# Latent products of a hybrid diffusion block: the order of the high-weight and low-weight matmuls

## The chip, the cores and the metric

The kernel runs on one core of one Trainium2 chip. The metric is the device time of one execution in microseconds. Before the change it was 2398.35 us, the median of three runs (2396.97 to 2398.81).

## The reference, cut to what matters

One layer of a diffusion backbone works on 256 latent tokens and 256 context tokens, D_MODEL = 2048. A token mixer (a bidirectional Mamba-2 scan with a gate z, a Conformer branch, two branch gates, an output projection) is followed by a SwiGLU FFN with 5632 hidden channels. Only the latent stream is returned.

```python
proj = h @ w_in                     # h: (b, L, 2048); columns z | x, B, C | dt | glu | gates
...
y_a = rmsnorm(y * jax.nn.silu(z), ssm_norm) @ w_proj_a            # 4096 -> 2048
u, v = jnp.split(glu, 2, axis=-1)
cf = jax.nn.silu(layernorm(cf_conv(u * jax.nn.sigmoid(v)), cf_ln_g, cf_ln_b))
y_b = cf @ w_proj_b                                               # 2048 -> 2048
out = (jax.nn.sigmoid(g_a) * y_a + jax.nn.sigmoid(g_b) * y_b) @ w_out
...
def swiglu(h, w_gate, w_up, w_down):
    return (jax.nn.silu(h @ w_gate) * (h @ w_up)) @ w_down        # 2048 -> 5632 -> 2048
```

All inputs are float32. The products that the change touches are those of the latent tokens alone: the columns z, glu and gates of `w_in`, and `w_proj_a`, `w_proj_b`, `w_ffn_gate`, `w_ffn_up`.

## The kernel before, in words

**Three products for one.** TensorE works on float32r operands. A float32 product is made of three: weights and activations are each split into a rounded part (high) and the remainder (low), and high x high, high x low and low x high are added up. An activation tile holds both parts side by side, `[P, k, 2, 256]`: 256 tokens high, then 256 tokens low.

**A unit of weights.** `unit_cols` (line 118) loads 512 KB: four k-tiles (`UK` = 4, 128 rows each) by 256 output columns. SP issues the DMA into a float32 tile w (6 buffers). `split` (line 110) then lets ACT round it into the tile wh (line 114; the high weights, 4 buffers) and DVE subtract to the tile wl (line 115; the low weights, 4 buffers). Both are emitted with the priority of an instruction 450 places earlier.

**A product with the weights stationary.** `mm_unit` (line 132, its branch for `wd` = 0) does, for each of the two 128-column halves j of a unit: four matmuls with a high weight tile, each over 512 columns (256 tokens high, 256 tokens low; line 152), then four with a low weight tile over the 256 columns of the high activations (line 154). The two results of one output half stand in one PSUM bank, columns 0 to 255 and 256 to 511. In the last unit of a product the last high matmul is held back to the end of the half (line 156). Each matmul has a weight load of its own. In the text below, H is a matmul of lines 152 and 156 and lo is one of line 154; a unit is thus H4 lo4 into one bank and H4 lo4 into the next.

**The end of a product.** `fold` (line 200) takes a bank out: an ACT copy of the one half (line 203), then a DVE add of the other half (line 204). Only then is the bank free. There are four such banks (`accp`, line 78), taken in turn in pairs by `acc2()`.

**Where such products run.** `zpair` (line 743) and `gpair` (line 788) lie between the steps of the scan (about 240 to 970 us); after each unit they yield, and the scan puts its own steps there. `pair` (line 846) does the glu columns, the rest of the gates, `w_proj_b` and `w_proj_a` (about 970 to 1540 us; the first two column groups of `w_proj_a` in a loop of their own, line 970). In all of these the next product takes the other two banks. In the FFN (line 1060, about 1655 to 2144 us) a group j of 256 hidden channels takes all four banks: two for the gate (ag), two for the up product (au), and their units alternate: gate, up, gate, up, eight units to a group. The first group does its gate product in another way (`mm_half`). `xpair` and `bcpair` (512-column matmuls throughout, but for the C half) and `chunks` (`w_out`, `w_down`: activations stationary, lines 174 to 177) are other forms.

**What sets the order.** A planner sorts the instructions while it builds the program: on each engine it takes, of those that are ready in its own account of time, the one with the earliest priority. On the chip each engine then runs its list strictly in that order. Behind every unit a `hook` (line 565) may emit a step of `modvec` (line 519), a background job on DVE (lines 533 to 537, tile mac) that multiplies and adds rows of `w_mod` as their DMAs come.

## Time and profile before

| | before |
|---|---|
| median of 3 runs | 2398.35 us |
| the profiled execution's own time | 2399.29 us |
| its span (first to last instruction) | 2397.6 us |
| mean granted TensorE clock | 0.994 |
| PE busy | 2337.8 us, 98% |
| PE weight loads busy | 1968.7 us, 82% |
| DVE busy | 1633.7 us, 68% |
| ACT busy | 1252.8 us, 52% |

PE is TensorE's matmul row and PEld its weight-load row. Matmuls are pipelined, so the busy time of PE is a union of overlapping rows; what a matmul costs in a stream is the distance from its start to the next one's start, not its own duration. The distances below are taken so.

### The profile page before, as it was taken

The page shows a single profiled execution, that of the slowest core. Times are in us where ns is not written, and L with a number is a line of the kernel's source. Part 1 is how long each engine was busy: PE and PEld are TensorE (multiplying, and loading weights), DVE is VectorE, ACT ScalarE, POOL GpSimd, SP SyncE. Part 2 cuts the span into 40 slices and gives each one's busy share as a digit, 9 for nine tenths or more (in the row PEclk, how much of TensorE's full clock was granted, in tenths as well). Part 3 has the DMA queues.
Part 4 walks back from the last instruction along what each step waited for, and adds up shares of the span by engine and source line. Part 5 has one row for each costly group of instructions (what it writes and reads, how often), then busy time and mean ns, then how long its engine had stood idle before and what let it go on. Part 6 is the DMA issues. An engine that isn't in the chain of part 4 may idle for free.

```text
span 2397.6 us, 34659 instructions
## 1 busy us (share of the span) xinstructions
PE 2337.8 (98%) x13180; PEld 1968.7 (82%) x13180; DVE 1633.7 (68%) x2099; ACT 1252.8 (52%) x1934; POOL 126.9 (5%) x149
## 2 busy tenths in 40 slices
PE   6899999999999999999999999998999999999998
PEld 3668788888888788888888888888888888888888
DVE  4559867676676776889878776767666566655554
ACT  4335766666566675654575444445444444444433
POOL 1000000100000000011300000000000000000000
PEclk9999999999999999999999999999999999999999
DMA  9884545546455566888799987885777677767553
GB/s 276 273 272 135 134 133 150 159 134 159 131 150 162 147 189 192 280 254 284 227 286 300 287 275 249 299 289 169 224 230 222 214 226 225 227 201 247 194 193 115
DMA packets 444848, 510.46 MB, mean 213 GB/s; under 512 B 17944, under 2 KB 391927, under 8 KB 443529
## 3 DMA queue, kind: packets, MB, share of 16 engines
q1 hardware_dynamic: 438904, 488.75, 66.7%
q0 software_dynamic: 5216, 18.41, 2.2%
q8 instruction: 103, 1.69, 0.3%
q10 hardware_dynamic: 560, 1.08, 0.1%
q14 instruction: 65, 0.52, 0.1%
HBM read 499.51 MB, written 8.67 MB: 212 GB/s over the span
## 4 chain that ended last, share of the span: by engine, by line
PE 89%; DMA 5%; DVE 2%; ACT 2%; issue 1%; SPq 1%; DVEq 0%; ACTq 0%
PE acc L152 34%; PE acc L154 18%; PE acc L144 6%; PE acc L145 5%; PE acc L147 5%; PE acc L177 4%; PE acc L174 4%; PE acc L175 4%; DMA w<-in_w_mod_dram 3%; PE acc L156 2%; DMA w<-in_w_in_dram 2%; PE ss L716 1%; PE ss L413 1%; DMA cs<-cs_d 1%; PE ss L686 1%
## 5 line engine op out<-in xcount | busy, mean ns | idle before, releaser
L115 DVE TENSOR_TENSOR wl<-w,wh 128x1024 fp32r<-128x1024 f32 (+3 forms) x702 | 847.1, 1210 | 486.6 <-ACT wh L114 484.4
L114 ACT CAST wh<-w 128x1024 fp32r<-128x1024 f32 (+3 forms) x702 | 717.7, 1024 | 742.2 <-PE acc L152 349.6
L152 PE MATMUL acc<-hx,wh 128*128 128x512 f32 x1556 | 433.0, 397 | 0.0
L152 PE MATMUL acc<-h,wh 128*128 128x512 f32 x1290 | 356.6, 395 | 1.9 <-DVE fe L204 1.9
L152 PEld LDWEIGHTS acc<-hx,wh 128*128 128x128 f32 x1556 | 271.9, 189 | 40.8 <-issue 2.2
L154 PEld LDWEIGHTS acc<-hx,wl 128*128 128x128 f32 x1664 | 254.8, 188 | 37.6 <-DVE wl L115 2.1
L144 PE MATMUL acc<-hx,wh 128*128 128x512 f32 x656 | 266.3, 407 | 3.0 <-ACT wh L114 2.6
L154 PE MATMUL acc<-hx,wl 128*128 128x256 f32 x1664 | 265.1, 281 | 1.4 <-DVE wl L115 1.4
L145 PE MATMUL acc<-hx,wh 128*128 128x512 f32 x656 | 259.2, 395 | 0.2 <-DVE hx L440 0.2
L152 PEld LDWEIGHTS acc<-h,wh 128*128 128x128 f32 x1290 | 225.5, 189 | 34.0 <-DVE fe L204 2.6
L154 PEld LDWEIGHTS acc<-h,wl 128*128 128x128 f32 x1376 | 211.5, 189 | 29.7
L537 DVE SCALAR_TENSOR_TENSOR mac<-w,silc,mac 128x1024 f32<-128x1024 f32 x120 | 154.7, 1289 | 104.7 <-DMA w<-in_w_mod_dram 104.0
L154 PE MATMUL acc<-h,wl 128*128 128x256 f32 x1376 | 219.5, 281 | 0.0
L147 PE MATMUL acc<-hx,wl 128*128 128x512 f32 x656 | 183.2, 392 | 0.0
L144 PEld LDWEIGHTS acc<-hx,wh 128*128 128x128 f32 x656 | 124.2, 189 | 38.1 <-ACT wh L114 8.2
L175 PE MATMUL acc<-wh,hid 128*128 128x512 f32 (+1 forms) x440 | 146.8, 347 | 0.0
L174 PE MATMUL acc<-wh,hid 128*128 128x512 f32 (+1 forms) x440 | 146.8, 347 | 0.0
L145 PEld LDWEIGHTS acc<-hx,wh 128*128 128x128 f32 x656 | 124.3, 190 | 26.3 <-issue 1.4
L147 PEld LDWEIGHTS acc<-hx,wl 128*128 128x128 f32 x656 | 123.3, 188 | 27.2 <-issue 0.7
L152 PE MATMUL acc<-yg,wh 128*128 128x512 f32 x496 | 136.3, 395 | 0.0
L177 PE MATMUL acc<-wl,hid 128*128 128x512 f32 (+1 forms) x440 | 109.5, 347 | 0.0
L667 ACT ACTIVATE cs<-cs,ncs 128x128 f32<-128x128 f32 x256 | 81.6, 390 | 34.6 <-DMA cs<-cs_d 30.9
(331 smaller groups left out, 2795.0 us busy)
## 6 DMA issues: line engine op xcount, KB each, us to landing
w<-in_w_in_dram SPq DMA_DIRECT2D x248, 512.0 KB, 4.5
w<-in_w_mod_dram SPq DMA_DIRECT2D x192, 512.0 KB, 4.8
w<-in_w_ffn_gate_dram SPq DMA_DIRECT2D x88, 512.0 KB, 4.5
w<-in_w_ffn_up_dram SPq DMA_DIRECT2D x88, 512.0 KB, 4.5
w<-in_w_ffn_down_dram SPq DMA_DIRECT2D x88, 512.0 KB, 3.7
w<-in_w_proj_a_dram SPq DMA_DIRECT2D x64, 512.0 KB, 5.0
w<-in_w_in_dram SPq DMA_DIRECT2D x74, 256.0 KB, 3.8
cs<-cs_d SPq DMA_DIRECT2D x32, 512.0 KB, 5.8
```

What stands on the lines that cost most here:

```text
L114: A.copy(out=hi[:, :n], in_=t[:, :n])
L115: V.tensor_tensor(out=lo[:, :n], in0=t[:, :n], in1=hi[:, :n].bitcast(F32), op=ALU.subtract)
L144: E.matmul(o, wj(hi, k), act(kofs + k)[:, 0, :ncol], start=kofs + k == kbeg, stop=False)
L145: E.matmul(o, wj(hi, k), act(kofs + k)[:, 1, :ncol], start=False, stop=False)
L147: E.matmul(o, wj(lo, k), act(kofs + k)[:, 0, :ncol], start=False, stop=last and k == nk - 1)
L152: E.matmul(o2, wj(hi, k), act(kofs + k)[:, :, :T], start=kofs + k == kbeg, stop=False)
L154: E.matmul(o[:, :T], wj(lo, k), act(kofs + k)[:, 0, :T], start=False, stop=last and not hold)
L174: E.matmul(o, act(kofs + k)[:, 0, s], hi[:, k], start=kofs + k == 0, stop=False)
L175: E.matmul(o, act(kofs + k)[:, 1, s], hi[:, k], start=False, stop=False)
L177: E.matmul(o, act(kofs + k)[:, 0, s], lo[:, k], start=False, stop=kofs + k == kend - 1)
L537: V.scalar_tensor_tensor(out=ac, in0=wt, scalar=silc[:, k - 1:k], in1=ac, op0=ALU.mult, op1=ALU.add)
L667: A.activation(out=t4[:, r, j], in_=t4[:, r, j], func=AF.Identity, bias=ncs[:, cc, r * 64 + hs + j:r * 64 + hs + j + 1])
```

## The change

Two units are taken together. `mm_run` emits all H of the first unit (both halves), then all H of the second, then all lo of the first and of the second, then the held-back H of those units that end their product. In a product of one pair of banks (`cols_run`: z, glu, gates, `w_proj_b`, `w_proj_a`) the two units are neighbours in k; in the FFN they are the gate's and the up product's unit of the same k. Both units are loaded and split before the first matmul. The generator yields once ahead of the second unit's H and once at the end, so the number of yields and hooks stays the same; in the FFN both hooks stand behind the run. `xpair`, `bcpair`, `chunks`, the context stage and the first FFN group's gate keep their order.

```diff
+    def mm_run(us, kend, act):
+        def wide(a, j, hi, k, kk):
+            E.matmul(a[j].rearrange("p (h t) -> p h t", h=2), hi[:, k, j * P:(j + 1) * P], act(kk)[:, :, :T],
+                     start=kk == 0, stop=kk == kend - 1)
+        for n, (a, hi, lo, kofs) in enumerate(us):
+            if n == len(us) - 1:
+                yield
+            for j in range(2):
+                for k in range(UK):
+                    if kofs + k < kend - 1:
+                        wide(a, j, hi, k, kofs + k)
+        for a, hi, lo, kofs in us:
+            for j in range(2):
+                for k in range(UK):
+                    E.matmul(a[j][:, :T], lo[:, k, j * P:(j + 1) * P], act(kofs + k)[:, 0, :T], start=False, stop=False)
+        for a, hi, lo, kofs in us:
+            if kofs + UK == kend:
+                for j in range(2):
+                    wide(a, j, hi, UK - 1, kend - 1)
+
+    def cols_run(a, w, c0, ktot, act):
+        for k0 in range(0, ktot, 2 * UK):
+            us = [(a, *unit_cols(w, k, UK, [(c0, 256)]), k) for k in (k0, k0 + UK)]
+            yield from mm_run(us, ktot, act)
+            yield
...
         def zpair(g, j, res):
             a = acc2()
-            for k0 in range(0, KD, UK):
-                hi, lo = unit_cols(w_in, k0, UK, [(g * 512 + j * 256, 256)])
-                mm_unit(a, hi, lo, UK, k0, KD, [0, 0], hxa)
-                yield
+            yield from cols_run(a, w_in, g * 512 + j * 256, KD, hxa)
...
-    def pair(w, c0, ktot, act, hook=None, whole=0):
+    def pair(w, c0, ktot, act, hook):
         a = acc2()
-        for k in range(0, ktot, UK):
-            m = min(UK, ktot - k)
-            hi, lo = unit_cols(w, k, m, [(c0, 256)])
-            mm_unit(a, hi, lo, m, k, ktot, [whole] * 2, act, ncol=T if whole else 512)
-            if hook is not None:
-                hook()
+        for _ in cols_run(a, w, c0, ktot, act):
+            hook()
         return a
...
         first = [acc2(), acc2()]
         for k0 in (0, KD):
             for j in range(2):
-                for k in range(k0, k0 + KD, UK):
-                    hi, lo = unit_cols(w_pa, k, UK, [(j * 256, 256)])
-                    mm_unit(first[j], hi, lo, UK, k, 2 * KD, [0, 0], yact)
+                for k in range(k0, k0 + KD, 2 * UK):
+                    us = [(first[j], *unit_cols(w_pa, kk, UK, [(j * 256, 256)]), kk) for kk in (k, k + UK)]
+                    for _ in mm_run(us, 2 * KD, yact):
+                        hook()
                     hook()
...
             for k0 in range(0, KD, UK):
-                for w, a in ((w_gate, ag), (w_up, au)):
-                    if j or a is au:
-                        hi, lo = unit_cols(w, k0, UK, [(j * 256, 256)])
-                        mm_unit(a, hi, lo, UK, k0, KD, [0, 0], h2a)
-                        hook()
+                us = [(a, *unit_cols(w, k0, UK, [(j * 256, 256)]), k0)
+                      for w, a in ((w_gate, ag), (w_up, au)) if j or a is au]
+                for _ in mm_run(us, KD, h2a):
+                    pass
+                for _ in us:
+                    hook()
```

`gpair` changes as `zpair` does.

## Rows read from the trace of the kernel before

**Rows 1.** The page: the busy time of each engine (us, share of the span, number of instructions).
```profile
PE 2337.8 (98%) x13180; PEld 1968.7 (82%) x13180; DVE 1633.7 (68%) x2099; ACT 1252.8 (52%) x1934; POOL 126.9 (5%) x149
```
**Rows 2.** The page: the chain of work that ended last, by engine.
```profile
PE 89%; DMA 5%; DVE 2%; ACT 2%; issue 1%; SPq 1%; DVEq 0%; ACTq 0%
```
**Rows 3.** The timeline of PE at the end of one FFN group and the start of the next (start us, us, engine, line, operation, out<-in, form, count): the last matmul of each of the four banks, the next group's first, and the last matmul of the first bank one group later.
```profile
1892.00 0.39 PE L156 MATMUL acc<-h,wh 128*128 128x512 f32 x1
1893.40 0.39 PE L156 MATMUL acc<-h,wh 128*128 128x512 f32 x1
1894.80 0.39 PE L156 MATMUL acc<-h,wh 128*128 128x512 f32 x1
1896.20 0.39 PE L156 MATMUL acc<-h,wh 128*128 128x512 f32 x1
1896.43 1.09 PE L152 MATMUL acc<-h,wh 128*128 128x512 f32 x4
1897.36 0.63 PE L154 MATMUL acc<-h,wl 128*128 128x256 f32 x4
...
1914.44 0.39 PE L156 MATMUL acc<-h,wh 128*128 128x512 f32 x1
```
**Rows 4.** The timeline of PE in an `xpair` product: 512-column matmuls in a row, long after the last shorter one.
```profile
781.67 0.39 PE L145 MATMUL acc<-hx,wh 128*128 128x512 f32 x1
...
786.43 0.39 PE L152 MATMUL acc<-hx,wh 128*128 128x512 f32 x1
```
**Rows 5.** The same in another `xpair` product, just behind four 128-column transposes; of the rows between, each is one 512-column matmul.
```profile
404.04 0.60 PE L607 MATMUL tp<-ident,xc 128*128 128x128 f32 x4
404.39 0.48 PE L144 MATMUL acc<-hx,wh 128*128 128x512 f32 x1
404.71 0.39 PE L145 MATMUL acc<-hx,wh 128*128 128x512 f32 x1
...
406.10 0.39 PE L145 MATMUL acc<-hx,wh 128*128 128x512 f32 x1
406.33 0.85 PE L147 MATMUL acc<-hx,wl 128*128 128x512 f32 x3
```
**Rows 6.** The timeline of PE in the last chunk of `w_down`: 256-column matmuls in a long row.
```profile
2378.27 0.28 PE L174 MATMUL acc<-wh,hid 128*128 128x256 f32 x1
...
2379.23 0.64 PE L177 MATMUL acc<-wl,hid 128*128 128x256 f32 x4
```
**Rows 7.** The timeline of ACT over the group boundary of rows 3 (in brackets: idle time before it, and what ended it).
```profile
1892.43 0.37 ACT L203 COPY fe<-acc 128x256 f32<-128x256 f32 x1 [0.83 <-PE acc L156]
1893.83 1.05 ACT L114 CAST wh<-w 128x1024 fp32r<-128x1024 f32 x1 [1.03 <-PE acc L156]
1894.78 0.82 ACT L203 COPY fe<-acc 128x256 f32<-128x256 f32 x2
1896.51 0.64 ACT L1078 ACTIVATE fe<-fe 128x512 f32<-128x512 f32 x1 [0.90 <-DVE fe L204]
1897.04 1.04 ACT L114 CAST wh<-w 128x1024 fp32r<-128x1024 f32 x1
1897.98 0.36 ACT L203 COPY fe<-acc 128x256 f32<-128x256 f32 x1
```
**Rows 8.** The timeline of DVE over the same boundary.
```profile
1892.84 0.42 DVE L204 TENSOR_TENSOR fe<-fe,acc 128x256 f32<-128x256 f32 x1
1894.91 1.23 DVE L115 TENSOR_TENSOR wl<-w,wh 128x1024 fp32r<-128x1024 f32 x1 [1.66 <-ACT wh L114]
1896.06 0.75 DVE L204 TENSOR_TENSOR fe<-fe,acc 128x256 f32<-128x256 f32 x2
1896.72 1.28 DVE L537 SCALAR_TENSOR_TENSOR mac<-w,silc,mac 128x1024 f32<-128x1024 f32 x1
1898.11 1.23 DVE L115 TENSOR_TENSOR wl<-w,wh 128x1024 fp32r<-128x1024 f32 x1
1899.26 0.41 DVE L204 TENSOR_TENSOR fe<-fe,acc 128x256 f32<-128x256 f32 x1
```
**Rows 9.** Who waited for whom, 1660 to 2150 us (us in total, times, longest): PE's one line, and ACT's longest.
```profile
PE acc L152 <- DVE fe L204: 1.9, 1, 1.9
...
ACT wh L114 <- PE acc L152: 161.7, 103, 2.2
```
**Rows 10.** That one wait, between the FFN's first two groups: DVE, PE, and the granted clock by stretch (start:end, us, busy of PE, PEld, DVE, ACT, POOL, then the clock, DMA share, GB/s).
```profile
1670.77 1.29 DVE L537 SCALAR_TENSOR_TENSOR mac<-w,silc,mac 128x1024 f32<-128x1024 f32 x1 [1.63 <-DMA w<-in_w_mod_dram]
1671.97 0.41 DVE L204 TENSOR_TENSOR fe<-fe,acc 128x256 f32<-128x256 f32 x1
...
1667.53 1.09 PE L152 MATMUL acc<-h,wh 128*128 128x512 f32 x4
...
1672.44 1.19 PE L152 MATMUL acc<-h,wh 128*128 128x512 f32 x4 [1.95 <-DVE fe L204]
...
1672.50:1676.00 3.50, 3.50 (x13) 2.94 (x14) 3.47 (x5) 0.62 (x1) 0.00 (x0) 0.66 0.89 290
```
**Rows 11.** The timeline of PE at the start of `w_proj_b`, where the order that the program was written in would be H4 lo4 H4 lo4.
```profile
1268.43 1.62 PE L152 MATMUL acc<-cfx,wh 128*128 128x512 f32 x6 [2.63 <-DVE cfx L945]
1269.89 0.65 PE L154 MATMUL acc<-cfx,wl 128*128 128x256 f32 x4
1270.38 0.63 PE L152 MATMUL acc<-cfx,wh 128*128 128x512 f32 x2
1270.84 0.63 PE L154 MATMUL acc<-cfx,wl 128*128 128x256 f32 x4
```
**Rows 12.** Groups of instructions on DVE from 1667 to 2144 us: the background job's three lines (count, busy us, mean ns, idle before them).
```profile
L537 DVE SCALAR_TENSOR_TENSOR mac<-w,silc,mac 128x1024 f32<-128x1024 f32 x29 | 37.2, 1284 | 25.5 <-DMA w<-in_w_mod_dram 25.3
...
L535 DVE TENSOR_TENSOR mac<-mac,w 1x1024 f32<-1x1024 f32 x1 | 1.2, 1206 | 0.0
L533 DVE TENSOR_SCALAR mac<-w,silc 128x1024 f32<-128x1024 f32 x1 | 0.8, 755 | 1.1 <-DMA gr_d<-mac 1.1
```
**Rows 13.** PE's waits in the scan stage, 240 to 970 us, the four longest.
```profile
PE ss L686 <- DVE cs L679: 2.1, 2, 1.8
PE tp L607 <- ACT btok L629: 1.0, 1, 1.0
PE ss L686 <- PE acc L145: 0.8, 1, 0.8
PE ss L716 <- DVE y L722: 0.3, 1, 0.3
```

More of the change, by code (lines that the diff above doesn't have):

```diff
@@ L790, in gpair @@
             a = acc2()
-            for k0 in range(0, KD, UK):
-                hi, lo = unit_cols(w_in, k0, UK, [(OFF_GLU + j * 256, 256)])
-                mm_unit(a, hi, lo, UK, k0, KD, [0, 0], hxa)
-                yield
+            yield from cols_run(a, w_in, OFF_GLU + j * 256, KD, hxa)
             early.append(fold(a, xct().rearrange("p (i t) -> p i t", i=2)))
```

## The prediction

> **What bounds the kernel now.** I read the page first: PE is busy 98% of the span, no other engine over 82%, and PE's weight loads are on the same engine [rows 1]. The chain that ended last says the same: PE 89%, DMA 5% [rows 2]. So a microsecond of PE's stream is a microsecond of the end, and nothing else counts unless it makes PE wait. Then I looked in the timeline at how far apart matmuls start. One FFN group is 8 units, 22.44 us from its last matmul into the first bank to the same one a group later (1892.00 to 1914.44), so an H4 lo4 takes 22.44 / 16 = 1.4025 us, of which H4 0.93 and lo4 0.47 (1896.43, 1897.36, and the rest) [rows 3]: 0.2325 us for an H and 0.118 for a lo. A 512-column matmul in a long row of its kind is cheaper: 21 starts in 4.76 us, 0.2267 each [rows 4]. Just behind short matmuls it is dear again: the seven steps from 404.71 to 406.33 take 0.231 each [rows 5]. So the H are slowed by some 0.005 us each for a number of matmuls behind shorter ones; the row 5 stretch spans the first nine, row 4 shows it gone. Lo have no such reserve: 256-column matmuls in a long row start every 0.120 us (eight in 0.96) [rows 6], no faster than in runs of four.
>
> Next, the waits. In the FFN PE waited once in 490 us, 1.9 us for a fold's add; ACT meanwhile waited 161.7 us for PE to give its buffers back [rows 9]. So weights are always ready early, and what can make PE wait there is the bank that the next group needs.
>
> **Part 1: longer runs.** Units: z 16, early gates 5, glu 16 and late gates 11 products of 4 units; `w_proj_b` 8 of 4, `w_proj_a` 8 of 8; FFN 22 x 8, less the 4 units that the first gate does in another way: 192 + 32 + 64 + 172 = 460. Four are alone in the first FFN group, so 228 runs of two. Before, two units are 4 x 0.93 = 3.72 us of H and 4 x 0.4725 = 1.89 of lo. After, the first ten H of a run cost 0.2314 and the last six 0.2267: 3.674. The 16 lo cost 16 x 0.118 = 1.89, or 1.92 at the row of long runs; I take the middle, 1.905. That is -0.046 + 0.015 = -0.031, times 228 = **-7 us**. Bounds: only four H slowed and lo as now, 4 x 0.2325 + 12 x 0.2267 = 3.65, -0.07 a run, -16 us; all H slowed and lo at 0.120, +0.03 a run, +7 us.
>
> At this place the Trainium skill speaks against the change: "TensorE: Matmul & The Clock Gate", section Back-to-back issue gap, lets the gap of a warm matmul follow from its columns alone (N / 2.4 plus 2.5 ns: an estimate of 216 ns for 512 columns and 109 for 256), with no cost for what ran before. The rows say 227 to 233 and 118 to 120, and that what ran before does matter; by the rule part 1 is 0.
>
> **Part 2: the FFN's group boundary.** Before, the gate's banks were finished 4.43 and 3.03 us ahead of the next group's first matmul and the up banks 1.63 and 0.23 ahead, and each bank was asked for again only 0, 1.4, 2.8 and 4.2 us behind it [rows 3]. After the change the four held-back H come last, one behind the other: g0, g1, u0, u1 start 0.93, 0.70, 0.47 and 0.23 before T, the time at which the next group could start, and it asks for g0 at T, g1 at T + 0.93, u0 at 1.86, u1 at 2.8.
>
> A fold is, from rows 7 and 8: copy 0.43 behind the start of the last matmul (1892.00, 1892.43), 0.37 long, add 0.04 later, 0.42 long; PE starts 0.06 after an add (1671.97 + 0.41 to 1672.44) [rows 10]. So g0 is free at T - 0.93 + 0.43 + 0.37 + 0.04 + 0.42 + 0.06 = T + 0.39: **0.39 us** of waiting that nothing covers, since all four banks are held.
>
> For g1 look at the order on ACT. A cast wh and a copy are released by the same matmul (1893.40 + 0.43); the cast goes first (1893.83), the copy 0.95 later; DVE likewise puts wl (1894.91) ahead of the adds (1896.06), each wl taking 1.15 of it [rows 7, 8]. After: the cast for the second next run's gate unit is released with g1 at T - 0.27, starts behind g0's copy at T - 0.13; by its end the up unit's cast is released too (T + 0.20) and goes from 0.82 to 1.77; only then g1's copy, 1.77 to 2.14. On DVE the first wl starts at T + 0.96, the second at 2.11, the add at 3.26; g1 is free at T + 3.74. PE has done g0's H4 at T + 1.32. The planner fills such holes with what is ready: at 1268.43 it ran H6 lo4 H2 lo4 where the program has H4 lo4 H4 lo4 [rows 11]. Ready are g0's lo4, and g0's H4 and lo4 of the following run: 0.47 + 0.93 + 0.47 = 1.87, to T + 3.19. So **0.55 us** is left; the sum is 0.94. Without filling it is 0.39 + 2.42 = 2.8.
>
> Between T and T + 3.74 DVE's list has no slack now. The background job puts 31 steps into 477 us, 39.2 us busy and 26.6 waiting for their DMA, all of it ahead of the adds behind them [rows 12]: one in each 15.4 us, thus in a quarter of the boundaries, 39.2 / 31 + 26.6 / 31 = 2.1 us each, half of which the 0.64 us hole ahead of the first wl and PE's filling may take: **+0.25**. Together 1.2 us a boundary; bounds 0.39 (copies and adds all go first) and 2.8 + 0.5 = 3.3.
>
> There are 20 boundaries between the second and the last group and one into `w_down`, whose first chunk takes g0 and g1: 21 x 1.2 = 25. Between the first two groups the up banks are asked for at 1.87 us behind 1667.53 and not at 2.81; that wait already ended last (1671.97 behind a step of the background job, rows 10), so it grows by up to 0.9: +0.9. **Sum +26 us**; bounds 21 x 0.39 = 8 and 21 x 3.3 + 0.9 = 70.
>
> **Parts that I cost at nothing.** Elsewhere the next product takes the other two banks and has a whole product (four units, 11.2 us) for its folds; were that cover gone, each product would pay part 2's 0.39. Loads and splits: hi of a unit is given back earlier (8 H, 1.86 us, not 2.3), lo up to 1.9 us later, against 1.27 for a wl; the 161.7 us that ACT waits for PE [rows 9] hide it. The same DMAs are issued by SP in the same order. The scan's steps move by up to 0.9 us; PE waits there 4.2 us in all [rows 13], so at best -4, and as much the other way.
>
> **Sum.** -7 + 26 = +19 on the profiled 2399.29 (its span and 1.7 us around it): 2418. The median lies 0.94 below: **2417 us**.
>
> **Rivals.**
> A. Folds go first: each boundary costs 0.39, 8 us, against -7: 2399. For it: at the row boundary g0's copy met an idle ACT. Against: rows 7 and 8 show casts and wl taken ahead of released copies and adds.
> B. Faster: the run length pays in full, -16, and the boundaries cost the same 8: 2390. It decides as soon as a boundary costs less than 1/21 of what the runs give, 0.35 us at -7 and 0.76 at -16. For it: row 4 shows 0.2267 as the steady step. Against: the slow steps of row 5 last nine matmuls, and after four H the next short ones come.
> C. PE's list isn't filled: 21 x 2.8 + 0.9 - 7 = +53: 2451. Worse, a wait may lower the clock: behind the 1.95 us wait the stretch from 1672.5 has a granted clock of 0.66, matmuls partly at the lower level of 1.2 GHz [rows 10], 34% of 3.5 us lost, 1.2 us; at half of the boundaries 12 us more. For it: PE stood idle in that wait and ran nothing else. Against: rows 11.
> D. The order of columns does nothing on PE, part 1 is 0: 2398 + 26 = 2424. For it: H and lo cost almost as much as in any long row; against: rows 4 and 5. By the skill's rule above, the time is this one.
>
> **How the numbers follow.** Forecast 0.43 (own range 2406 to 2430, from 0.9 to 1.5 us a boundary and 0 to -12 of runs), A 0.17, B 0.13, C 0.19, D 0.08. This kernel can be told from no change by about 0.2%, 4.8 us: A is the same, B faster, the rest slower; with a share of B's neighbours faster 0.15, same 0.17, slower 0.68. The range leaves out half of B at the low end and half of C at the high one: 2392 to 2446.
>
> **What would show it.** In the FFN a group of 8 units takes 22.44 - 0.13 + 1.2, about 23.5 us; the waits name the add of line 204 as PE's releaser some 40 times, 0.4 us before g0 and 0.5 before g1; ACT's casts stand between g0's and g1's copies. Elsewhere two units take 5.58 us, not 5.61, with H steps of 0.227 at the end of a run. I am wrong if PE shows no wait at line 204 (then the banks come free in time), or if the steps in a run of 16 stay at 0.2325.

## The result and the profile after

The changed kernel takes **2435.96 us** (median of five runs, 2426.22 to 2437.90) against 2396.97 us (five runs, 2393.63 to 2398.81) of the kernel before, timed beside it: the ratio is 1.0148, 95% interval 1.0131 to 1.0165. It is slower, by 39 us between the medians and by 31 to 40 us by the interval. The prediction was 2417 us, in a range from 2392 to 2446: the sign and about half of the loss were foreseen, some 19 us of it were not.

The profiled execution of after took 2429.82 us, which is below its median and 30.5 us above the profiled one of before. All sums below are made between these two, so they account for 30.5 us and not for the whole of 39. From the page of after, the span, then the busy times [rows 1], then the chain that ended last [rows 2]:

```profile
span 2428.0 us, 34750 instructions
...
PE 2348.5 (97%) x13180; PEld 1973.9 (81%) x13180; DVE 1623.9 (67%) x2099; ACT 1239.1 (51%) x1934; POOL 120.3 (5%) x149
...
PE 77%; DMA 8%; issue 7%; DVE 5%; ACT 2%; SPq 0%; DVEq 0%; ACTq 0%; POOL 0%; POOLq 0%
```

The number of matmuls is the same. PE is busy 10.7 us longer and idle 19.7 us longer. These rows can't say where, but the chain hints at the kind: DMA, DVE and "issue" now have 20% of it and had 8%.

To find the place, take the first matmul of each stage. From the timeline of PE of the kernel before (start us, us, engine, line, operation, out<-in, form, count); the first row is the first product matmul behind the scan's last step, and `w_proj_b` begins at 1268.43 [rows 11]:

```profile
929.12 0.48 PE L152 MATMUL acc<-hx,wh 128*128 128x512 f32 x1
...
1358.45 0.62 PE L152 MATMUL acc<-yg,wh 128*128 128x512 f32 x2
...
1539.92 0.40 PE L174 MATMUL acc<-wh,mx 128*128 128x512 f32 x1
...
1656.29 0.44 PE L152 MATMUL acc<-h,wh 128*128 128x512 f32 x1
...
2144.01 0.39 PE L174 MATMUL acc<-wh,hid 128*128 128x512 f32 x1
```

The same of the kernel after, where H are line 162, lo line 174, a fold's copy line 232 and its add line 233:

```profile
924.36 0.48 PE L162 MATMUL acc<-hx,wh 128*128 128x512 f32 x1
...
1270.95 0.47 PE L162 MATMUL acc<-cfx,wh 128*128 128x512 f32 x1 [4.30 <-DVE cfx L964]
...
1364.96 0.62 PE L162 MATMUL acc<-yg,wh 128*128 128x512 f32 x2
...
1549.57 0.39 PE L203 MATMUL acc<-wh,mx 128*128 128x512 f32 x1
...
1665.88 0.44 PE L162 MATMUL acc<-h,wh 128*128 128x512 f32 x1
...
2174.30 0.50 PE L203 MATMUL acc<-wh,hid 128*128 128x512 f32 x1 [0.22 <-DVE fe L233]
```

The differences of these starts are the stage lengths, in us:

| stage | before | after | change |
|---|---|---|---|
| context and scan | 929.12 | 924.36 | -4.8 |
| glu and late gates | 339.31 | 346.59 | +7.3 |
| `w_proj_b` | 90.02 | 94.01 | +4.0 |
| `w_proj_a` | 181.47 | 184.61 | +3.1 |
| `w_out` and the first FFN gate | 116.37 | 116.31 | -0.1 |
| FFN | 487.72 | 508.42 | +20.7 |
| `w_down` and the end | 253.6 | 253.7 | +0.1 |

So two places lose, the FFN 20.7 us and the three stages between scan and `w_out` 14.4 us. These are single executions, and two rows can't be read finer than some microseconds. The 4.8 us of context and scan are no gain that is shown: `e11`, `e6` and `e3` below run the order of before there and take 921.9, 924.2 and 925.6 us, and the six-tile kernels with two-unit runs there take from 923.4 to 927.3. Nor is it shown that `w_out` loses nothing: `e10`, `e2` and `e1` have the code of after from there to the FFN and take 119.7, 121.4 and 121.8 us for the 116.31 here.

**The runs themselves gain.** From the start of the first H of a run of 16 to the first lo is 3.654 us (median over the FFN's unbroken runs), 16 lo take 1.913: 5.567 us for two units, where before they took 5.61 [rows 3]. That is some 0.042 us less a run, which a group of four runs without a loss confirms (22.27 us in `e2` below, 22.44 before). The H steps of a run are 0.233, 0.236, 0.228, 0.233, 0.231 and then 0.227 eleven times, so the slow ones are the first five.

**The FFN's boundary.** PE between two groups of after, undisturbed by the background job:

```profile
1772.51 1.09 PE L162 MATMUL acc<-h,wh 128*128 128x512 f32 x4
1773.82 1.20 PE L162 MATMUL acc<-h,wh 128*128 128x512 f32 x4 [0.22 <-DVE fe L233]
1774.86 0.63 PE L174 MATMUL acc<-h,wl 128*128 128x256 f32 x4
1775.33 1.08 PE L162 MATMUL acc<-h,wh 128*128 128x512 f32 x4
1776.25 0.63 PE L174 MATMUL acc<-h,wl 128*128 128x256 f32 x4
1777.04 3.01 PE L162 MATMUL acc<-h,wh 128*128 128x512 f32 x12 [0.16 <-DVE fe L233]
```

The first row is the four held-back H, one for each bank. With 0.23 each they end their stream at T = 1773.44. The next H comes 0.38 us later, and then the planner's filling, H4 lo4 H4 lo4, all into the first bank (of this run and of the next), instead of 16 H. It ends at 1776.72, and the second bank's first H starts 0.32 later still. ACT and DVE over the same stretch:

```profile
1772.94 0.37 ACT L232 COPY fe<-acc 128x256 f32<-128x256 f32 x1 [5.75 <-PE acc L162]
1773.21 2.00 ACT L114 CAST wh<-w 128x1024 fp32r<-128x1024 f32 x2
1775.11 0.92 ACT L232 COPY fe<-acc 128x256 f32<-128x256 f32 x3
```
```profile
1773.35 0.42 DVE L233 TENSOR_TENSOR fe<-fe,acc 128x256 f32<-128x256 f32 x1 [3.84 <-ACT fe L232]
1774.30 2.36 DVE L115 TENSOR_TENSOR wl<-w,wh 128x1024 fp32r<-128x1024 f32 x2 [0.53 <-ACT wh L114]
1776.57 1.08 DVE L233 TENSOR_TENSOR fe<-fe,acc 128x256 f32<-128x256 f32 x3
```

Read it by the order: ACT takes one copy, then two casts of weights that are needed a run later, and then the three copies that the next matmuls need; DVE one add, two wl, three adds. In rows 7 and 8 the same order stood there and cost nothing, since the banks then came one by one with 1.4 us between them.

**The background job at a boundary.** Between 1913 and 1920 us one of its steps stands ahead of the first add. DVE, then PE, then the clock by stretch (start:end, us, busy of PE, PEld, DVE, ACT, POOL, granted clock, DMA share, GB/s):

```profile
1914.88 1.28 DVE L566 SCALAR_TENSOR_TENSOR mac<-w,silc,mac 128x1024 f32<-128x1024 f32 x1 [4.83 <-DMA w<-in_w_mod_dram]
1916.08 0.41 DVE L233 TENSOR_TENSOR fe<-fe,acc 128x256 f32<-128x256 f32 x1
```
```profile
1916.54 1.96 PE L162 MATMUL acc<-h,wh 128*128 128x512 f32 x4 [2.40 <-DVE fe L233]
```
```profile
1914.00:1916.60 2.60, 0.20 (x2) 0.06 (x1) 1.73 (x3) 2.57 (x5) 0.00 (x0) 1.00 0.33 110
1916.80:1920.00 3.20, 3.20 (x10) 2.63 (x10) 3.10 (x6) 0.63 (x1) 0.00 (x0) 0.50 0.68 189
1921.00:1935.00 14.00, 14.00 (x83) 12.37 (x82) 7.35 (x7) 6.82 (x7) 0.00 (x0) 1.00 0.65 201
```

PE waits 2.40 us, and the matmuls behind that wait run at a granted clock of 0.50, TensorE's lower level of 1.2 GHz. This group takes 26.53 us where an undisturbed one takes 23.22.

**Between the scan and `w_out`.** Who waited, of ACT, from 970 to 1550 us, before and then after (us in total, times, longest). The loss here was not in the prediction.

```profile
ACT wh L114 <- PE acc L152: 123.9, 85, 2.1
ACT wh L114 <- PE acc L156: 30.1, 29, 1.1
ACT wh L114 <- DMA w<-in_w_in_dram: 17.4, 13, 4.0
```
```profile
ACT wh L114 <- PE acc L162: 64.3, 45, 3.0
ACT wh L114 <- DMA w<-in_w_in_dram: 35.5, 25, 3.5
...
ACT wh L114 <- DMA w<-in_w_proj_b_dram: 16.1, 11, 4.9
```

And PE in the same stretch of after; before it has 2.6 for cfx and 1.4 for a wl, 4.0 us in all:

```profile
PE acc L174 <- DVE wl L115: 6.9, 7, 2.3
PE acc L162 <- DVE cfx L964: 4.3, 1, 4.3
PE acc L162 <- ACT wh L114: 3.1, 3, 2.1
```

ACT waits 64.3 us for PE to give buffers back where it was 154.0, and longer for weights to land: 35.5 us for those of `w_in` where it was 17.4. PE then waits 14.3 us where it was 4.0, and 10.0 of it are for splits (wl and wh) where that was 1.4. The worst place is the one ahead of `w_proj_b`, in DVE's timeline of after:

```profile
1261.59 1.29 DVE L566 SCALAR_TENSOR_TENSOR mac<-w,silc,mac 128x1024 f32<-128x1024 f32 x1 [4.21 <-DMA w<-in_w_mod_dram]
1262.79 0.41 DVE L233 TENSOR_TENSOR gb<-gb,acc 128x256 f32<-128x256 f32 x1
```

and in PE's:

```profile
1262.11 1.11 PE L174 MATMUL acc<-hx,wl 128*128 128x256 f32 x8
1264.39 1.22 PE L174 MATMUL acc<-hx,wl 128*128 128x256 f32 x8 [1.17 <-DVE wl L115]
```

A row of the job came late, 4.21 us of DVE went by, and folds, wl and in the end cfx were late behind it; PE's 4.30 us wait at 1270.95 closes the chain. The lower clock stands behind the longer waits of after here too, as the clock by stretch shows for the place behind 1270.95:

```profile
1271.60:1275.00 3.40, 3.40 (x10) 2.62 (x9) 2.55 (x5) 1.84 (x4) 0.00 (x0) 0.50 1.04 377
```

Two more such stretches of 3.4 to 3.5 us lie at 1186.2 and 1384.2, behind waits of 2.33 and 2.06 us. The kernel before has no such stretch in these three stages. Three times half of 3.4 is 5 us (an estimate, for matmuls at half the clock); with the 10.3 us of added waits that makes 15 of the 18.7 us lost here (14.4, and 102 runs of two units that should have gained 0.042 each). The other 3 us are not placed.

### The profile page after: what moved, and what is told of

Its sections match the earlier page's. It is cut to its first block, busy times and chain, and to the rows that moved or that the text cites. A ratio compares the mean times of both kernels' runs of the same rounds, so it can differ in the third digit from the quotient of the medians.

```text
span 2428.0 us, 34750 instructions
## 1 busy us (share of the span) xinstructions
PE 2348.5 (97%) x13180; PEld 1973.9 (81%) x13180; DVE 1623.9 (67%) x2099; ACT 1239.1 (51%) x1934; POOL 120.3 (5%) x149
## 4 chain that ended last, share of the span: by engine, by line
PE 77%; DMA 8%; issue 7%; DVE 5%; ACT 2%; SPq 0%; DVEq 0%; ACTq 0%; POOL 0%; POOLq 0%
PE acc L162 26%; PE acc L174 13%; PE acc L144 6%; PE acc L145 5%; PE acc L147 5%; DMA w<-in_w_mod_dram 5%; PE acc L206 4%; PE acc L203 4%; PE acc L204 4%; DVE wl L115 2%; ACT wh L114 1%; PE acc L152 1%; PE ss L745 1%; DMA cs<-cs_d 1%; PE ss L442 1%
## 5 line engine op out<-in xcount | busy, mean ns | idle before, releaser
L115 DVE TENSOR_TENSOR wl<-w,wh 128x1024 fp32r<-128x1024 f32 (+3 forms) x702 | 832.0, 1206 | 408.1 <-ACT wh L114 289.2
L162 PE MATMUL acc<-hx,wh 128*128 128x512 f32 x1536 | 376.7, 394 | 0.8 <-ACT wh L114 0.8
L162 PE MATMUL acc<-h,wh 128*128 128x512 f32 x1376 | 346.6, 397 | 13.7 <-DVE fe L233 13.3
L162 PEld LDWEIGHTS acc<-h,wh 128*128 128x128 f32 x1376 | 249.8, 190 | 71.5 <-DVE fe L233 26.2
L144 PE MATMUL acc<-hx,wh 128*128 128x512 f32 x656 | 265.9, 406 | 2.5 <-ACT wh L114 2.1
L145 PE MATMUL acc<-hx,wh 128*128 128x512 f32 x656 | 259.1, 395 | 0.2 <-DVE hx L469 0.2
L174 PEld LDWEIGHTS acc<-hx,wl 128*128 128x128 f32 x1536 | 198.3, 192 | 14.2 <-DVE wl L115 6.6
L174 PE MATMUL acc<-hx,wl 128*128 128x256 f32 x1536 | 202.2, 284 | 5.0 <-DVE wl L115 4.9
L174 PEld LDWEIGHTS acc<-h,wl 128*128 128x128 f32 x1376 | 182.5, 191 | 10.5
L174 PE MATMUL acc<-h,wl 128*128 128x256 f32 x1376 | 185.6, 283 | 0.0
L147 PEld LDWEIGHTS acc<-hx,wl 128*128 128x128 f32 x656 | 123.6, 189 | 27.3 <-issue 0.7
L162 PE MATMUL acc<-yg,wh 128*128 128x512 f32 x512 | 125.2, 396 | 2.3 <-ACT wh L114 2.3
L162 PEld LDWEIGHTS acc<-yg,wh 128*128 128x128 f32 x512 | 94.9, 190 | 22.0 <-ACT wh L114 2.7
```

The lines of the kernel that those rows point to most:

```text
L115: V.tensor_tensor(out=lo[:, :n], in0=t[:, :n], in1=hi[:, :n].bitcast(F32), op=ALU.subtract)
L144: E.matmul(o, wj(hi, k), act(kofs + k)[:, 0, :ncol], start=kofs + k == kbeg, stop=False)
L145: E.matmul(o, wj(hi, k), act(kofs + k)[:, 1, :ncol], start=False, stop=False)
L147: E.matmul(o, wj(lo, k), act(kofs + k)[:, 0, :ncol], start=False, stop=last and k == nk - 1)
L162: E.matmul(a[j].rearrange("p (h t) -> p h t", h=2), hi[:, k, j * P:(j + 1) * P], act(kk)[:, :, :T], start=kk == 0, stop=kk == kend - 1)
L174: E.matmul(a[j][:, :T], lo[:, k, j * P:(j + 1) * P], act(kofs + k)[:, 0, :T], start=False, stop=False)
```

## The experiments

Three theories stood at the start. *Boundary*: the FFN's four banks finished together cost what Part 2 says. *Buffers*: the loss between scan and `w_out` comes from weights that are split later and from buffers that are given back later. *Rows*: long runs are as dear as short ones, and nothing else is to be had. Stage lengths are read as in the table above, from each kernel's profiled execution; ratios are to the kernel before, run beside it.

### Undoing the FFN's part

`e1` is the kernel after with the FFN's loop of before.

```diff
-                us = [(a, *unit_cols(w, k0, UK, [(j * 256, 256)]), k0)
-                      for w, a in ((w_gate, ag), (w_up, au)) if j or a is au]
-                for _ in mm_run(us, KD, h2a):
-                    pass
-                for _ in us:
-                    hook()
+                for w, a in ((w_gate, ag), (w_up, au)):
+                    if j or a is au:
+                        hi, lo = unit_cols(w, k0, UK, [(j * 256, 256)])
+                        mm_unit(a, hi, lo, UK, k0, KD, [0, 0], h2a)
+                        hook()
```

> The changed kernel with the FFN's group loop put back to H4 lo4 per bank, gate and up units in turn. Theory (the FFN loses at its group boundaries, because the four banks are finished together): the FFN from its first 512-column matmul to w_down goes back from 508.4 us to 487.7, within 1 us; the whole kernel is some 21 us faster than the changed one and still 10 to 18 us slower than the one before (970 to 1550 us stays about 14 us longer). Rival (waits just shift along and the loss of one stage reappears in another): the total stays within 8 us of the changed kernel.

Measured: 2415.55 us, ratio 1.0079 (1.0062 to 1.0096); the FFN takes 486.3 us, 1.4 below the 487.7 that was expected, and waits for a fold once, 1.9 us, as before [rows 9]. So the FFN's part is worth some 20 us, and what is left of the change still costs 16. Part 1 alone, with the boundary away, would have been a gain of 4 us by the prediction's working: something outside the FFN is dearer than it said.

### Long runs in the FFN with the banks staggered

`e2` is the kernel after with FFN runs of two neighbours in k, of the gate and then of the up product, so that gate and up banks again end a run apart. `e3` has this in the FFN and the kernel before everywhere else.

```diff
-            for k0 in range(0, KD, UK):
-                us = [(a, *unit_cols(w, k0, UK, [(j * 256, 256)]), k0)
-                      for w, a in ((w_gate, ag), (w_up, au)) if j or a is au]
-                for _ in mm_run(us, KD, h2a):
-                    pass
-                for _ in us:
-                    hook()
+            for k0 in range(0, KD, 2 * UK):
+                for w, a in ((w_gate, ag), (w_up, au)):
+                    if j or a is au:
+                        us = [(a, *unit_cols(w, k, UK, [(j * 256, 256)]), k) for k in (k0, k0 + UK)]
+                        for _ in mm_run(us, KD, h2a):
+                            hook()
+                        hook()
```

> The changed kernel, but in the FFN a run takes two units of one product, neighbours in k (gate, gate, then up, up), so runs are as long as in the change while the gate's banks are finished 5.6 us ahead of the group's end. Theory (bank release, not run length, costs the FFN its 20.7 us): the FFN takes 487.7 - 86 x 0.042 = 484 us (483 to 487), PE waits at most a few times for a fold's add there. Rival (long runs themselves starve PE of weights in the FFN): 495 us or more, with waits on the casts of lines 114 and 115.

> The kernel before with long runs in the FFN alone, two units of one product to a run. Theory: every other stage as before, the FFN at 484 us, the whole 3 to 4 us faster than before (2393 to 2395 beside 2397). Rival (the step of a run is not shorter when measured over the whole): within 1.5 us of before.

Measured: `e2` 2408.20 us, ratio 1.0047 (1.0032 to 1.0062); `e3` 2393.55 us, ratio 0.9978 (0.9969 to 0.9988), which is faster than the kernel before, by 0.2% and clear of 1. The FFN takes 480.96 and 481.4 us, less than the 483 to 487 that were expected, and a group 22.27 us: the long runs are kept, and the boundary costs nothing. In `e2` PE's waits for a fold from 1660 to 2150 us are

```profile
PE acc L162 <- DVE fe L233: 0.3, 1, 0.3
```

against 13.3 us in 29 waits in after. Of the 6.3 us that `e3`'s FFN wins, 3.6 are 86 runs by 0.042 (here the four units of the first group run in pairs too); most of the rest is the first boundary (22.87 us for the group in `e2`, 23.30 in `e3`, 26.14 in before, 22.27 for an undisturbed one); the same loop as before took 24.69 there in `e1`, so that part is not steady. So the length of the runs is no loss by itself, and *Rows* falls. `e2` and `e3` differ only outside the FFN, where long runs cost 14.65 us of the medians.

### Runs of one unit

`e4` takes one unit per run, H8 lo8, in all the places that the change touches (the loops of `w_proj_a` and of the FFN are edited alike, and `mm_run` no longer yields).

```diff
-        for k0 in range(0, ktot, 2 * UK):
-            us = [(a, *unit_cols(w, k, UK, [(c0, 256)]), k) for k in (k0, k0 + UK)]
-            yield from mm_run(us, ktot, act)
-            yield
+        for k0 in range(0, ktot, UK):
+            mm_run([(a, *unit_cols(w, k0, UK, [(c0, 256)]), k0)], ktot, act)
+            yield
...
```

> Runs of one unit everywhere: H8 lo8 per unit, gate and up units in turn, held-back H of both banks at the unit's end. By the steps measured in the changed kernel an H8 takes 233 + 236 + 228 + 233 + 231 + 3 x 227 = 1.842 us for 2 x 0.929, a lo8 0.952 for 2 x 0.473: 10 ns a unit, 460 units, 4.6 us less. Theory (what costs is what is held to the end of a two-unit run: the banks in the FFN, the low weights and their float32 tiles from 970 to 1550 us): the FFN takes 486 us (485 to 489), the stretch from 970 to 1550 us is within 4 us of before, the whole 0 to 6 us faster than before. Rival (any order other than H4 lo4 upsets that stretch): it is 10 us or more longer than before.

Measured: 2398.95 us, ratio 1.0003 (0.9993 to 1.0013). The three stages take 337.8, 91.3 and 185.3 us: 3.6 us above before in sum where after was 14.4. A group of the FFN takes 22.35 us, half of the gain that a pair's runs give. On the whole there is no difference, where the theory had 0 to 6 us less. The stages fit *Buffers*, as only one unit at a time holds its low buffers, and for no longer than its own run.

### Is it the background job?

The float32 tile w of a unit is free again once its wl is made, and wl needs a low buffer, which comes free only at the end of a two-unit run. The job's rows of `w_mod` use the same six tiles. If that is the mechanism, long runs cost nothing where the job is absent. `e5` (from `e2`) and `e6` (from `e3`) run 40 of the job's steps in the glu and gates, none in the loops of `w_proj_b` and `w_proj_a`, and 68 in `w_out` (six of these run ahead, into the last 15 us of `w_proj_a`).

```diff
-    hook = bg(mgen, 108, 226)
+    hook = bg(mgen, 40, 108)
...
+        hook = lambda: None
         mps = ExitStack()
...
-        chunks(w_out, KD, lambda k: mx[:, k], epi, hook, split=True)
+        chunks(w_out, KD, lambda k: mx[:, k], epi, bg(mgen, 68, 32), split=True)
```

> As the second experiment (long runs everywhere, FFN pairs in k), but the background job puts no step into the products of w_proj_b and w_proj_a: its first 40 steps go to the glu and gates products, the rest to w_out. There the stretch from the first w_proj_b matmul to w_out took 93.9 + 186.4 = 280.3 us in the second experiment and 91.6 + 181.5 = 273.1 with H4 lo4. Theory (the job's row loads take float32 tiles that the split weights now hold longer, and its steps hold up DVE): without the job the long runs are at or below its H4 lo4 twin of this call, by 0 to 2 us (48 runs x 0.042). Rival (the stage's own folds and splits collide): still 4 us or more above the twin.

> The twin of the run before with H4 lo4 outside the FFN. Both theories: w_proj_b and w_proj_a together 268 to 272 us (64 + 32 units at 2.805 us are 269).

Measured, `w_proj_b` and `w_proj_a` together: long 90.76 + 178.13 = 268.9 us, short 89.75 + 179.52 = 269.3. With the job they are 93.93 + 186.39 = 280.3 (`e2`) and 91.58 + 181.47 = 273.1 (`e3`). So without the job the long runs cost 0.4 us less than the short ones, with it 7.2 more. A stretch at the lower clock behind the first wait of `w_proj_b` (from 1262.8 us; the mean clock from 1262 to 1360 us is 0.98) is in the 268.9 us, and none (1.00) is in the 269.3; at some 1.7 us for it, the long runs come to the 2.0 us less that 48 of them should give. PE waits for nothing in either between 1270 and 1530 us. In the glu and gates the pair shows that the job's mere presence does not decide: with its steps thinned from about 52 to 40, long runs take 337.5 us and short ones 343.2, where they took 347.6 (`e2`) and 339.5 (`e3`). Which of its steps do the harm there was not tried. The whole times say nothing here, 2436.00 and 2445.48 us: the 68 steps crowd `w_out`, which takes 150.5 and 148.4 us in place of some 100.

### One more float32 tile

The other way to test it: leave the job and add a tile. `e7` (from `e2`) and `e8` (from `e3`) have seven, paid for with one buffer fewer of five work tiles.

```diff
-NW32, NWH, NWL = 6, 4, 4
+NW32, NWH, NWL = 7, 4, 4
...
-        return pa1.tile([P, 512], F32, tag="xc", name="xc", bufs=9)
+        return pa1.tile([P, 512], F32, tag="xc", name="xc", bufs=8)
...
-                xw = ptile([P, 512], "xw", 2)
+                xw = ptile([P, 512], "xw", 1)
```

> The second experiment with a seventh float32 weight tile, paid for by smaller work tiles elsewhere (one h32, xc, xw, fc and xn tile fewer, the same in the twin). Theory (too few float32 tiles, since a unit's tile is held until its low weights may be made): the stretch from the scan's end to the FFN, 17 us longer than the H4 lo4 kernel's in the second experiment, is less than 8 us longer than the twin's. Rival (the order on DVE or the four low buffers): still 13 us or more longer than the twin's.

> The twin of the run before with H4 lo4 outside the FFN and seven float32 tiles. Both theories: the stretch from the scan's end to the FFN within 5 us of the third experiment's; the whole within 8 us of it (smaller work tiles may cost some in the scan).

Measured: 2399.30 us, ratio 0.9994 (0.9979 to 1.0008), and 2394.87 us, 0.9978 (0.9966 to 0.9991). From the scan's end to the FFN's first 512-column matmul the twins take 739.8 and 736.7 us, 3.1 apart; with six tiles they were 749.4 and 731.7, 17.7 apart. PE's waits of `e7` from 970 to 1550 us:

```profile
PE acc L162 <- DVE cfx L964: 3.9, 1, 3.9
PE acc L174 <- DVE wl L115: 3.1, 2, 2.6
PE acc L162 <- ACT wh L114: 1.7, 2, 1.2
```

In the three stages alone, `e7` takes 615.2 us and `e8` 614.4, 0.8 apart, where `e2` and `e3` (628.0 and 612.5) were 15.4 apart. The other 2.3 of the 3.1 us lie in `w_out` and the first FFN gate, where the twins run the same code and where such differences come without one (see the table). So the seventh tile takes away nearly all of the long runs' loss, and no wait of ACT for a weight's DMA is left among its seven longest. It brings no gain beyond that: `e8` is no faster than `e3`, and context and scan take 928.9 us in `e7` and 923.9 in `e8`, 5.5 more and 1.7 less than in `e2` and `e3`. So for these stages the theory *Buffers* holds: float32 tiles were short, and the job that shares them matters. Whether more low buffers would have served as well was not tried.

### The best of both, and two more about the boundary

`e9` keeps long runs where they cost nothing, in the scan's products (z and early gates) and in the FFN by pairs of k, and takes H4 lo4 between scan and `w_out`. `e10` is the kernel after with the held-back H of a unit directly behind its own lo, so that the gate's banks end 8 lo ahead of the up banks:

```diff
         for a, hi, lo, kofs in us:
             for j in range(2):
                 for k in range(UK):
                     E.matmul(a[j][:, :T], lo[:, k, j * P:(j + 1) * P], act(kofs + k)[:, 0, :T], start=False, stop=False)
-        for a, hi, lo, kofs in us:
             if kofs + UK == kend:
```

`e11` is the kernel before with the change's FFN loop alone.

> Long runs in the scan's z and gate products and in the FFN (two units of one product), H4 lo4 in the products of 970 to 1540 us. Theory (that stretch loses, the scan and the FFN gain): 42 runs x 0.042 = 1.8 us less in the scan, the rest as in the third experiment; the whole 0 to 4 us below the third experiment's ratio, so 0.996 to 0.998 of before, and no slower than the third. Rival (the scan's own float32 tiles are short too): slower than the third experiment by 3 us or more.

> The changed kernel with one edit: a unit's held-back H follow its own lo, so that in a group's last run the gate's banks are finished before the up product's lo. The gate's last two H then start 1.88 and 1.65 us ahead of the next group instead of 0.93 and 0.70. By the order of part 2 the first bank is free 0.57 us before it is wanted, the second about 0.6 us late before PE's filling. Theory: the FFN takes 485 to 491 us beside 508.4, PE's waits for the fold's add mostly gone. Rival (the alternation of gate and up in one run is what costs): 500 us or more.

> The kernel before with the change's FFN loop alone. Theory (the two losses add up): the FFN 505 to 510 us, the whole 18 to 22 us slower than before (1.0075 to 1.0092), together with the first experiment's loss as much as the whole change. Rival (they overlap): less than 14 us.

Measured: `e9` 2393.72 us, ratio 0.9970 (0.9960 to 0.9981), FFN 482.3 us, context and scan together 927.3 us, inside the spread of that stage. Beside `e3` (0.9978) the intervals overlap, so a gain of the scan's long runs is not shown, nor a loss; both kernels beat the one before.

`e10` 2422.76 us, ratio 1.0096 (1.0081 to 1.0110). Its FFN, 496.7 us, lies between what the two expectations said. An undisturbed group takes 22.46 us, 0.19 above the 22.27 of `e2`: the boundary as such is nearly repaired. But where a step of the job comes, PE still waits. PE's waits from 1660 to 2180 us, of `e10`, and then the one behind the first group:

```profile
PE acc L162 <- DVE fe L232: 5.5, 5, 3.7
PE acc L174 <- DVE wl L115: 2.1, 1, 2.1
```
```profile
1685.89 1.28 DVE L565 SCALAR_TENSOR_TENSOR mac<-w,silc,mac 128x1024 f32<-128x1024 f32 x1 [2.05 <-DMA w<-in_w_mod_dram]
1687.09 0.41 DVE L232 TENSOR_TENSOR fe<-fe,acc 128x256 f32<-128x256 f32 x1
```

That add frees the bank that PE waits 3.75 us for, and the group takes 28.05 us. In the other long group, 27.31 us, a step of the job stands ahead of a wl, and PE waits 2.09 us for that and 0.82 for an add. So the order of four matmuls settles the regular loss of 0.8 us a group, and among these kernels only the pairs of k leave the job its room.

`e11` 2420.55 us, ratio 1.0086 (1.0071 to 1.0101): 21.3 us above its neighbour before, FFN 510.65, just above what was expected. With the 16.3 us of `e1` that makes 37.6, the whole change's loss within its interval: the two parts add up, as far as that interval tells.

## Why the prediction was right, and where it was short

**Bounds and sign.** Right. PE sets the end in both kernels, and the loss is PE's waiting in the places of the table.

**Part 1, longer runs.** Right in kind, a little small: -0.042 us a run and not -0.031. The ten slow H steps were five, with 0.227 from the sixth on, and lo are 0.1196 each, 1.913 us against the 1.905 taken. Over 228 runs, if all stayed whole, that is -9.6 us in place of -7. Rival D, part 1 is nothing, is out: a group of `e2` takes 22.27 us for 22.44. The page "TensorE: Matmul & The Clock Gate" of the Trainium skill (Back-to-back issue gap) would have it so by the formula that the prediction took from it, but it gives that formula for an isolated matmul and lets both operations set the spacing in a stream of weight loads and matmuls, which this kernel is. In this kernel's trace the step of an H goes from 0.236 to 0.227 us by what went before.

**Part 2, the boundary.** Right in its steps, and in its sum partly by luck. For an undisturbed group: 22.27 us without a loss, 23.22 with it, so 0.95 us a boundary where the text worked out 0.39 + 0.55 = 0.94. g0 came 0.38 us late; the second bank's first H stood 3.60 us behind T, where g1 was forecast free at 3.74; ACT took a copy, two casts, then three copies, DVE an add, two wl, then three adds; PE's list was filled with H4 lo4 H4 lo4. The pieces are shared out otherwise: 0.38 and 0.32 us by the distances of starts, 0.1 more in the H4 behind the first wait (1773.82 to 1774.86, 1.04 us where four H take 0.93), the rest, 0.15, in the broken runs. So the second wait was 0.2 us shorter than forecast, and 0.25 us for which the text had no term fill its place: that 0.94 meets 0.95 is chance. With the job, the 20 groups behind the first pair take 23.52 us on average, forecast 23.5, against 22.52 before: with the 0.17 that their runs gained, 1.17 us a boundary, forecast 1.2. Here too the mean is nearer than its parts: of the 20 groups six are disturbed, about the quarter that was forecast, but one of them (26.53 us) brings over half of the excess. The waits were said to be some 40, 0.4 and 0.5 us long; the profile has 30, 13.5 us, as it counts from the modelled end of the last matmul, so that 0.38 between streams shows as 0.22.

FFN in all: +26 forecast with 84 runs of -0.031, thus +23; measured +20.7. The first boundary was to cost 0.9 more; its group took 26.46 us against 26.14, which is inside what that group varies by (24.69 in `e1`).

**The rivals.** A, folds go first, fell: casts and wl stood in between. B, faster, fell with the boundary at 0.95 (its lower threshold, 7 / 21, is 0.33 us and not 0.35, which changes nothing). C fell in its main part, as PE's list was filled; its clock did come, but at two of the boundaries and not at half of them, one of which had it before the change too. Its price was read too low: the 0.66 of rows 10 is the mean of a window that starts 1.1 us ahead of the fall. The lower level itself stood at 0.50 for 3.4 us from 1673.63, as in the last row under the last heading, so half of 3.4, some 1.7 us, and not 1.2.

**The step that fell short** is the sentence "Loads and splits: ... the 161.7 us that ACT waits for PE [rows 9] hide it", among the parts costed at nothing. Rows 9 cover 1660 to 2150 us, the FFN. For the glu, gates, `w_proj_b` and `w_proj_a` the text took its cover from a stage that it was not read in. But the same number would have misled it there as well: in those stages ACT waited 154.0 us for PE before the change (first two rows of its waits above). A total of waits says nothing of the single loads that have no cover: beside it ACT waited 13 times for `w_in` to land before, 17.4 us, and in the FFN of before no such wait for a weight stands among its waits. In the three stages a step of the job stands behind nearly every second unit (91 of its DVE rows for 204 units, in the FFN 32 for 172), these rows wait 60.5 us for DMA before and 69.9 after, its tiles come from the same six, and DMA is busy 0.86 of the time against 0.72 in the FFN from 1690 to 2140. The text gave the right event, low buffers returned up to 1.9 us later, and compared it with the 1.27 us of a wl; but the chain does not end at the wl. A wl that starts late gives its float32 tile back late, SP issues the next load late, ACT waits for it (51.6 us in all for the two weights shown above, 22.8 before), and PE waits for the split. SP's queue agrees, though by little, in its waits for a wl from 970 to 1550 us, before and after:

```profile
SPq L107 <- DVE wl L115: 164.1, 120, 5.3
```
```profile
SPq L107 <- DVE wl L115: 179.9, 131, 8.1
```

It cost 18.7 us in these profiles, for which the sum had nothing. With -9.6 for all the runs, +24.2 for the boundaries (20.7, and the 3.5 that the FFN's runs gained), +18.7 for this and -3 by which context and scan came out shorter than their 42 runs explain, the sum is +30.3 where +19 was forecast. It meets the 30.5 us by which the profiled execution rose because the stage table adds up to that, and so proves nothing; the -3 lies in the spread of the scan. That the median rose by some 8 us more than the profiled execution is not explained. `e5` and `e6` (job away from `w_proj_b` and `w_proj_a`: no loss), `e7` and `e8` (a tile more: 0.8 us in place of 15.4 in the three stages) show the cause; the links of the chain, one by one, are argued from the timelines.

## What to carry to other kernels

A stretch of weights-stationary work that ends in several accumulators should end them one after another with at least a fold's length between: what was saved here by longer rows of one kind is worth 0.042 us a run, and one bank that was asked for too early cost 0.38, nine times that. Before you say that a delayed buffer is hidden, read the cover in every stage that the change touches, not in the longest one, look there for single loads that are already late, which a total of waits doesn't show, and follow the buffer to its last holder: here a two-step split holds the staging tile until its second step, and a background job draws on the same tiles. In the FFN a pairing that keeps accumulators staggered (neighbours in k) took the gain without the loss. And compare a stage over several executions before a few microseconds of it are called a gain.

## What was not expected of the hardware

- The price of going from short matmuls to long ones ends after five H (0.233, 0.236, 0.228, 0.233, 0.231, then 0.227), sooner than the ten that I took from rows 5; the first lo behind 16 H is quicker (0.113) than those after it (0.120).
- PE can pay for its waits twice. In after, behind each of the six waits of 2.06 to 4.30 us from 240 us on, the granted clock was 0.50 (1.2 GHz) for about 3.4 us, so that each such wait cost up to 1.7 us more (half of 3.4, an estimate); behind its waits of 1.72 us and less there was no such stretch. But the length of the wait does not settle it: in before the clock fell behind waits of 1.84 us (at 840.67) and 1.95 us (at 1672.44), and it stayed at 1.00 behind the 2.63 us ahead of `w_proj_b` at 1268.43. What does settle it these runs don't show. The stretches of before behind these three waits, in order of time:

```profile
840.80:844.10 3.30, 3.30 (x18) 2.87 (x19) 2.29 (x4) 2.54 (x6) 0.00 (x0) 0.50 0.78 245
1268.50:1272.00 3.50, 3.50 (x19) 3.00 (x20) 3.50 (x7) 3.30 (x6) 0.00 (x0) 1.00 0.97 354
1673.70:1677.00 3.30, 3.30 (x13) 2.91 (x12) 2.58 (x4) 1.45 (x2) 0.00 (x0) 0.50 0.86 277
```
